# Thirty-four DMA issues of an encoder layer's attention stage, begun by ScalarE instead of SyncE

## The chip, the core and the metric

The kernel is one program on one core of a Trainium2 chip. Its time is the device time of one launch in microseconds (us). The core has a matrix engine (TensorE: PE in the profile, PEld for its weight loads), VectorE (DVE), ScalarE (ACT), GpSimd (POOL) and SyncE (SP). SP computes nothing here: it begins transfers. Each engine works through its own instructions in their order, and an instruction that has to wait holds up all that stand behind it on that engine.

Matrices of weights and activations lie in DRAM. What the engines work on lies in SBUF, and matmuls write to PSUM banks. Whether an engine may go on is told by semaphores that other engines and finished transfers raise.

## What is computed

One layer of a transformer encoder on 1024 tokens of width 1024. Two attention branches of eight heads each (head size 64) are projected, gated, added and projected again. After a layer norm comes a gated feed-forward part.

```python
D_MODEL, SEQ, HEAD_DIM, N_HEADS_A, N_HEADS_B = 1024, 1024, 64, 8, 8
...
        h = x @ w_in[l]
        qa, ka, va, qb, kb, vb, ga, gb = jnp.split(h, split_pts, axis=-1)
        y_a = chunk_band_attention(heads_a(qa), heads_a(ka), heads_a(va), rel_bias[l]) @ w_proj_a[l]
        y_b = stick_breaking_attention(heads_b(qb), heads_b(kb), heads_b(vb)) @ w_proj_b[l]
        gate_a = jax.nn.sigmoid(ga + b_gate[l, :D])
        gate_b = jax.nn.sigmoid(gb + b_gate[l, D:])
        mix = (gate_a * y_a + gate_b * y_b) @ w_out[l]
        x = layer_norm(DEEPNORM_ALPHA * x + mix, ln1_g[l], ln1_b[l])
        g, u = jnp.split(x @ w_ffn_in[l], 2, axis=-1)
        x = layer_norm(DEEPNORM_ALPHA * x + (jax.nn.silu(g) * u) @ w_ffn_out[l], ln2_g[l], ln2_b[l])
```

Branch A is a softmax over a band of nine chunks of 64 keys with a learned bias. Branch B is stick-breaking: a weight is `sigmoid(z)` times the product of `1 - sigmoid(z)` over the keys between, found by a running product.

## The kernel before

All float32 products are made of three fp32r matmuls: each operand is split into a high part (a cast by ACT, L109) and the rest (a subtraction by DVE, L110). The program first projects `x` (to about 345 us of the span), then runs the attention stage (345 to 700 us), the second branch's projection with the output projection and a layer norm (to 830), and the feed-forward part.

**The attention stage** is the loop over `vsteps`: 16 heads (0 to 7 branch A, 8 to 15 branch B), each with 12 steps. A step is a turn (PE transposes up to four 128x128 blocks of weights into a bank `tp`, L561; ACT and DVE split them into `pt`, L109 and L110) and, two steps later, a multiplication (PE multiplies a block of values by `pt` and adds it up in `pv`, L574 and L575). There are three banks for `tp` (in branch B one of them holds the identity for the running products), one for `pv`, four `pt` slots and three `yt` slots. Between the steps the weights of coming heads are made: in branch A scores (L464, L465), bias and minimum on DVE (L495), `exp` on ACT (L500) and scaling on POOL (L503); in branch B two sigmoids on ACT (L528, L529), the running product on DVE (L532, L536) and a product on POOL (L538).

**A head's values** come out in two halves of 512 queries (`g` 0 and 1). Two neighbouring heads share a 128-row tile. After the last multiplication of a half, ACT copies the bank to SBUF (L589: 128x512). One transfer from SBUF to SBUF (L590: 64 rows of 512, 128 KB) brings the rows that belong to the other tile there. Three steps later, POOL adds them up (L593). After the fourth addition of a pair of heads SP stores the tile to `y_dr` (L595). The last pair (`i` = 7) does it otherwise (L581, L582), with no transfer.

**Filling work** is fed between the steps, by a price in matmuls: six gates (10 to 15, `gate()`, L421 on PE, copied by ACT at L424 and stored by one 512 KB transfer each, L425), then branch A's projection (`yAps`, L621). For the latter the stored values come back (`reload_y`: `yraw` by SP at L644, `yh` by ACT at L647, `yl` by POOL at L648), the gates too (`reload_gate`: `gA`, SP at L651, sigmoid by ACT at L653), and weights (`load_w`: SP at L403, ACT at L404, the rest at L405).

**What sets the order.** `dma` is `nc.sync.dma_start` (L83), so that SP begins every transfer before the change. The program is written in one sequence of steps, but a scheduler puts each engine's instructions in an order of its own, and it puts in the semaphore waits. A change to one engine's work therefore moves rows on the others.

Of the kernel before, what the change touches and what calls it, by code (L numbers as in the profile page):

```python
# [18 lines left out]
P = 128  # L19
# [3 lines left out]
DH = 64  # L23
# [24 lines left out]
def hybrid_trunk_kernel(ctx: ExitStack, tc, x, xt, w_in, b_gate, rel_bias, w_proj,  # L48
# [6 lines left out]
    nc = tc.nc  # L55
# [7 lines left out]
    def slot(tag, name, dtype=F32):  # L63
        return pool.tile([P, 1024], dtype, tag=tag, name=name, bufs=SLOTS[tag])
# [10 lines left out]
    def bank(tag, name):  # L75
        return ps.tile([P, HW], F32, tag=tag, name=name, bufs=BANKS[tag])

    def dram(name, n):
        return [dr.tile([P, 1024], F32, name=f"{name}{i}") for i in range(n)]
# [3 lines left out]
    dma = nc.sync.dma_start  # L83
# [13 lines left out]
    g_dr = dram("g_dr", 16)  # L97
# [10 lines left out]
    def split(dst_h, dst_l, src):  # L108
        nc.scalar.copy(dst_h, src)  # L109
        nc.vector.tensor_tensor(dst_l, src, dst_h.bitcast(F32), ALU.subtract)  # L110
# [303 lines left out]
    def gate(i, w):  # L414
        gt = slot("gt", f"gate{i}")
        for hf, cs in enumerate((LO, HI)):
            acc = bank("mm", f"gps{i}_{hf}")
            for k in range(KT):
                ks = slice(k * P, (k + 1) * P)
                for j, (lw, rx) in enumerate(((w[0], xh), (w[0], xl), (w[1], xh))):  # L420
                    mm(acc, lw[:, ks], rx[k][:, cs], start=(k == j == 0),  # L421
                       stop=(k == KT - 1 and j == 2))
                    yield 1.0
            nc.scalar.copy(gt[:, cs], acc)  # L424
        dma(g_dr[i], gt)  # L425

    left(2)
    take = project_plain(0)
# [113 lines left out]
    def value_steps(hd, g, wt):  # L542

        br, h = hd["br"], hd["h"]
        reach = (4, 8)[br]
        q0 = 4 * g
        nm = f"{'ab'[br]}{hd['n']}_{g}"
        pv = []

        kbs = [4, 5, 6, 7, 3, 2, 1, 0] if g == 0 else [7, 6, 5, 4]  # L550
        steps = []
        for i, kb in enumerate(kbs):
            lo_q = max(q0, kb - reach)
            hi_q = min(q0 + 3, kb)
            n = (hi_q - lo_q + 1) * P
            pts = []

            def turn(kb=kb, lo_q=lo_q, hi_q=hi_q, n=n, pts=pts):
                tp = bank("tr", f"tp_{nm}_{kb}")
                for qb in range(lo_q, hi_q + 1):  # L560
                    tr(tp[:, (qb - lo_q) * P:(qb - lo_q + 1) * P],  # L561
                       wt[qb - q0][:, (kb - qb) * P:(kb - qb + 1) * P], ident)
                pt = slot("pt", f"pt_{nm}_{kb}", F32R)
                split(pt[:, 0:n], pt[:, HW:HW + n], tp[:, 0:n])
                pts.append(pt)

            def mult(i=i, kb=kb, lo_q=lo_q, n=n, pts=pts):
                v = hd["v"]
                if i == 0:
                    pv.append(bank("pv", f"pv_{nm}"))  # L570
                last = i == len(kbs) - 1
                cs = slice((lo_q - q0) * P, (lo_q - q0) * P + n)
                pt = pts[0]
                mm(pv[0][:, cs], v[:, kb, :], pt[:, 0:n], start=(i == 0), stop=False)  # L574
                mm(pv[0][:, cs], v[:, kb, :], pt[:, HW:HW + n], start=False, stop=last)  # L575
                if last:
                    yt = hd["yt"]()
                    r = slice(h * DH, (h + 1) * DH)
                    gs = slice(g * HW, (g + 1) * HW)
                    if hd["i"] == 7:  # L580
                        nc.scalar.copy(yt[r, gs], pv[0][DH:P])  # L581
                        nc.vector.tensor_tensor(yt[r, gs], pv[0][0:DH], yt[r, gs], ALU.add)  # L582
                    else:

                        if g == 0:
                            hd["yv"] = slot("yt", f"yv_{nm}")
                        yv = hd["yv"]
                        both, other = (yt, yv) if h == 0 else (yv, yt)
                        nc.scalar.copy(both[:, gs], pv[0])  # L589
                        dma(other[r, gs], both[(DH, 0)[h]:(P, DH)[h], gs])  # L590

                        def add():
                            nc.gpsimd.tensor_tensor(yt[r, gs], yt[r, gs], yv[r, gs], ALU.add)  # L593
                            if h == 1 and g == 1:
                                dma(y_dr[hd["i"]], yt)  # L595
                        later.append([3, add])

            steps.append((turn, mult))
        return steps


    def fill_all():
        w = first_w
        for i in range(first_gate, 16):
            nxt = load_gate(i + 1, nc.gpsimd) if i < 15 else load_proj(0, 0, "op", nc.gpsimd)
            yield from gate(i, w)
            w = nxt
        for i in range(4):
            reload_y(i, nc.gpsimd)
        for cc in range(4):  # L610
            nxt = load_proj(0, cc + 1, "op", nc.gpsimd) if cc < 3 else None
            for j in range(2):
                c = 2 * cc + j
                t = slot("gt", f"gA{c}")
                reload_gate(t, c, 0)
                for hf, cs in enumerate((LO, HI)):
                    acc = bank("mm", f"yAps{c}_{hf}")
                    for k in range(4):
                        ks = slice(j * HW + k * P, j * HW + (k + 1) * P)
                        for n, (lw, rx) in enumerate(((w[0], yh), (w[0], yl), (w[1], yh))):  # L620
                            mm(acc, lw[:, ks], rx[k][:, cs], start=(k == n == 0),  # L621
                               stop=(k == 3 and n == 2))
                            yield 1.0
                    nc.vector.tensor_tensor(t[:, cs], acc, t[:, cs], ALU.mult)
                if c < KEEP:
                    dma(m_dr[c], t)
                else:
                    kept[c] = t
            if cc < 3:
                reload_y(4 + cc, nc.gpsimd)  # L630
            w = nxt
# [484 lines left out]
```

## Time and profile before

| what | value |
|---|---|
| time, median of 3 runs | 1467.64 us (1467.51 to 1469.79) |
| the profiled execution | 1466.33 us |
| its span in the profile | 1464.5 us |
| granted TensorE clock, mean | 0.997 |
| DVE busy | 1035.9 us (71%) |
| DMA | 247.72 MB, 169 GB/s mean |

The profiled execution is 1.31 us under the median. Between its time and its span lie 1.83 us. PE's share is the largest, and it is close to the whole span; so the readings below look for PE's idle time, stretch by stretch, and for what ended it.

### The profile page before, as it was taken

The numbers are of one execution on the slowest core, as the hardware profiler recorded it, in microseconds if no ns is written. First come the engines' busy times: TensorE is split into PE (matmuls) and PEld (weight loads), VectorE is DVE, ScalarE is ACT, GpSimd is POOL, SyncE is SP. The second block draws the span as 40 slices with busy tenths as digits, with TensorE's granted clock in tenths as the row PEclk, the third lists the DMA queues.
The fourth block names the chain that finished last, engine by engine and source line by source line (L and its number), as shares of the span: only waits on it lengthen the run. The fifth ranks groups of instructions, "written<-read, shape, count | busy, mean of one in ns | idle before, by whom it ended". The sixth has DMA issues, their size and how long they took to land.

```text
span 1464.5 us, 19170 instructions
## 1 busy us (share of the span) xinstructions
PE 1429.5 (98%) x6740; PEld 1181.3 (81%) x6740; DVE 1035.9 (71%) x1693; ACT 679.2 (46%) x1179; POOL 278.8 (19%) x326
## 2 busy tenths in 40 slices
PE   8999999999999998999999999999999999999997
PEld 6788888887888787777888888888888888888886
DVE  8856655434776987887848966777776665978767
ACT  6444444334887878775413534444444433221201
POOL 0000000003555779760004100000000000100016
PEclk9999999999999999999999999999999999999999
DMA  6555545328666476747611123444444456886602
GB/s 216 158 188 173 160 142 177 125 100 246 194 191 203 123 224 186 236 170 254 235 43 72 50 95 130 158 154 148 152 151 145 155 190 248 304 306 237 212 15 101
DMA packets 83455, 247.72 MB, mean 169 GB/s; under 512 B 10512, under 2 KB 10512, under 8 KB 83360
## 3 DMA queue, kind: packets, MB, share of 16 engines
q1 hardware_dynamic: 83360, 246.51, 50.6%
q8 instruction: 53, 0.87, 0.2%
q14 instruction: 42, 0.34, 0.1%
HBM read 162.03 MB, written 80.77 MB: 166 GB/s over the span
## 4 chain that ended last, share of the span: by engine, by line
PE 83%; DVE 7%; DMA 4%; ACT 2%; issue 2%; POOL 1%; SPq 0%; POOLq 0%; DVEq 0%; ACTq 0%
PE sxf L171 15%; PE sxp L171 12%; PE szf L171 8%; PE szp L171 6%; PE dx L1049 6%; PE syf L171 4%; PE gps L421 3%; PE dz L1049 3%; PE syp L171 3%; PE ops L119 2%; PE ops L117 2%; PE ops L116 2%; PE yAps L621 2%; PE dy L1049 1%; PE tp_b L561 1%
## 5 line engine op out<-in xcount | busy, mean ns | idle before, releaser
L1005 POOL TENSOR_TENSOR wdyt<-wdyt 128x512 f32<-128x512 f32 x8 | 10.9, 1366 | 513.6 <-DVE wdgt L1004 473.4
L538 POOL TENSOR_TENSOR w_b<-w_b,kp_b 128x511 f32<-128x511 f32 (+3 forms) x96 | 96.8, 1018 | 33.6 <-DVE kp_b L536 28.5
L536 DVE TENSOR_TENSOR_SCAN kp_b<-kp_b,ident_ps 128x384 f32<-128x384 f32 (+6 forms) x88 | 78.4, 891 | 7.0 <-ACT kp_b L528 2.2
L482 POOL MEMSET bias<- 64x64 f32 x8 | 1.2, 144 | 329.2 <-ACT bias L481 329.2
L184 DVE TENSOR_TENSOR c<-sxp,c 128x512 f32<-128x512 f32 x16 | 11.1, 692 | 74.6 <-issue 41.4
L769 POOL TENSOR_TENSOR mv<-mv,neghalf 128x1 f32<-128x1 f32 x16 | 23.8, 1489 | 209.4 <-DVE mv L768 209.4
L528 ACT ACTIVATE kp_b<-sc_b 128x512 f32<-128x512 f32 (+3 forms) x96 | 50.3, 525 | 24.0 <-PE sc_b L465 21.7
L110 DVE TENSOR_TENSOR pt_b<-tp_b,pt_b 128x512 fp32r<-128x512 f32 (+1 forms) x96 | 50.1, 541 | 12.5 <-ACT pt_b L109 12.3
L980 DVE TENSOR_TENSOR x<-dx,x 128x512 f32<-128x512 f32 x64 | 43.5, 687 | 17.0 <-PE dx L1049 16.9
L171 PE MATMUL szf<-x1S63h,wcf 128*128 128x512 f32 x168 | 55.1, 389 | 0.0
L109 ACT CAST pt_b<-tp_b 128x512 fp32r<-128x512 f32 (+1 forms) x96 | 48.4, 517 | 7.9 <-PE tp_b L561 7.3
L110 DVE TENSOR_TENSOR sl<-h,sl 128x512 fp32r<-128x512 f32 x56 | 38.4, 686 | 18.9 <-ACT sl L109 18.9
L503 POOL TENSOR_SCALAR w_a<-w_a,st_a 128x640 f32<-128x640 f32 (+2 forms) x64 | 42.6, 667 | 48.0 <-DVE st_a L502 29.7
L561 PE MATMUL tp_b<-ident,w_b 128*128 128x128 f32 x288 | 47.9, 275 | 3.4 <-DVE pt_b L110 3.1
L110 DVE TENSOR_TENSOR pt_a<-tp_a,pt_a 128x512 fp32r<-128x512 f32 (+1 forms) x96 | 46.0, 487 | 7.1 <-ACT pt_a L109 5.9
L529 ACT ACTIVATE w_b<-sc_b 128x511 f32<-128x511 f32 (+3 forms) x96 | 50.6, 527 | 0.0
L109 ACT CAST sl<-h 128x512 fp32r<-128x512 f32 x56 | 34.7, 619 | 33.5 <-PE syf L171 17.1
L116 PE MATMUL ops<-wh_o,mh 128*128 128x512 f32 x128 | 50.2, 392 | 0.0
L119 PE MATMUL ops<-wh_o,ml 128*128 128x512 f32 x128 | 50.0, 391 | 0.0
L117 PE MATMUL ops<-wl_o,mh 128*128 128x512 f32 x128 | 49.9, 390 | 0.0
L109 ACT CAST pt_a<-tp_a 128x512 fp32r<-128x512 f32 (+1 forms) x96 | 39.9, 425 | 19.2 <-PE tp_a L561 18.3
L500 ACT ACTIVATE w_a<-w_a,st_a 128x640 f32<-128x640 f32 (+2 forms) x64 | 44.7, 698 | 7.4 <-DVE st_a L495 5.7
(1883 smaller groups left out, 4796.5 us busy)
## 6 DMA issues: line engine op xcount, KB each, us to landing
s_dr<-sl SPq DMA_DIRECT2D x112, 256.0 KB, 2.2
sd<-s_dr SPq DMA_DIRECT2D x56, 512.0 KB, 4.8
wLf<-in_w_ffn_in_dram SPq DMA_DIRECT2D x22, 512.0 KB, 4.5
wRf<-in_w_ffn_in_dram SPq DMA_DIRECT2D x22, 512.0 KB, 3.5
wLp<-in_w_in_dram SPq DMA_DIRECT2D x17, 512.0 KB, 5.3
wRp<-in_w_in_dram SPq DMA_DIRECT2D x17, 512.0 KB, 4.2
v_dr<-v SPq DMA_DIRECT2D x16, 512.0 KB, 4.2
qs<-q_dr SPq DMA_DIRECT2D x16, 512.0 KB, 5.0
```

What stands on the lines that cost most here:

```text
L109: nc.scalar.copy(dst_h, src)
L110: nc.vector.tensor_tensor(dst_l, src, dst_h.bitcast(F32), ALU.subtract)
L116: mm(acc, lh, rh, start=(i == 0), stop=False)
L117: mm(acc, lh, rl, start=False, stop=False)
L119: mm(acc, ll, rh, start=False, stop=(i == n))
L171: mm(acc, lw[:, ks], rx, start=(first and kt == i == 0), stop=(kt == 3 and i == 2), skip_group_check=not first)
L528: nc.scalar.activation(kp[:, c0:e], sc[:, 0:n], AF.Sigmoid, scale=-1.0)
L529: nc.scalar.activation(be[:, m0:e], sc[:, m0 - c0:n], AF.Sigmoid)
L536: nc.vector.tensor_tensor_scan(kp[:, s0:e], kp[:, s0:e], ident_ps()[:, 0:e - s0], kp[:, s0 - 1:s0], ALU.mult, ALU.bypass)
L538: nc.gpsimd.tensor_tensor(be[:, m0:e], be[:, m0:e], kp[:, m0 - 1:e - 1], ALU.mult)
L561: tr(tp[:, (qb - lo_q) * P:(qb - lo_q + 1) * P], wt[qb - q0][:, (kb - qb) * P:(kb - qb + 1) * P], ident)
L1049: mm(acc, a, b, start=(first and i == n == 0), stop=(i == n - 1 == 1), skip_group_check=not first)
```

## The change

Two transfers are begun by ACT (`nc.scalar.dma_start`) instead of SP. The bytes, sources and targets are the same.

```diff
@@ gate(i, w)
             nc.scalar.copy(gt[:, cs], acc)
-        dma(g_dr[i], gt)
+        nc.scalar.dma_start(g_dr[i], gt)
@@ value_steps(hd, g, wt), mult()
                         nc.scalar.copy(both[:, gs], pv[0])
-                        dma(other[r, gs], both[(DH, 0)[h]:(P, DH)[h], gs])
+                        nc.scalar.dma_start(other[r, gs], both[(DH, 0)[h]:(P, DH)[h], gs])
```

That is 28 issues of L590 (seven pairs of heads, two heads, two halves) and 6 of L425. Each stands on ACT behind the copy that it reads, at once or a few rows later. SP keeps the stage's other transfers: queries, keys, values, weights, reloads and the remaining stores.

The scheduler's order changes on all engines from the first of these issues on. In the following rows a name ends in a number of its own for each tile; `a6`, `b4` are the head of branch A or B, `+` is a row of the changed kernel and `-` one of before.

ACT at the border of the branches: `w_a7` are the last softmax weights, `kp_b0` and `w_b0` the first sigmoids, and `yt3` holds the values of the pair of heads 6 and 7.

```order
 L500 ACTIVATE w_a7_1_1_4429,st_a7_6_4478<-w_a7_1_1_4429,st_a7_6_4478 128x256
 L589 COPY yt3_4424<-pv_a6_1_4445 128x512
+L590 DMA yv_a6_0_4425<-yt3_4424 64x512
+L500 ACTIVATE w_a7_1_1_4429,st_a7_7_4498<-w_a7_1_1_4429,st_a7_7_4498 128x128
 L528 ACT_TABLE_LOAD
 L528 ACTIVATE kp_b0_0_4510<-sc_b0_0_0_4512 128x512
-L500 ACT_TABLE_LOAD
-L500 ACTIVATE w_a7_1_1_4429,st_a7_7_4498<-w_a7_1_1_4429,st_a7_7_4498 128x128
-L529 ACT_TABLE_LOAD
 L529 ACTIVATE w_b0_0_0_4506<-sc_b0_0_0_4512 128x511
```

The last `exp` now stands ahead of the first sigmoid, so that two of three table loads are gone here.

POOL in head 11, where branch A's projection begins. Before, `yl2` and `yl3` (the rests of the reloaded values) stand ahead of the addition for `yt5`:

```order
L648 TENSOR_TENSOR yl2_5760<-yraw2_5757,yh2_5759 128x1024
L538 TENSOR_TENSOR w_b4_0_0_5653<-w_b4_0_0_5653,kp_b4_0_5657 128x511
L538 TENSOR_TENSOR w_b4_0_0_5653<-w_b4_0_0_5653,kp_b4_0_5657 128x512
L648 TENSOR_TENSOR yl3_5766<-yraw3_5763,yh3_5765 128x1024
L593 TENSOR_TENSOR yt5_5552<-yt5_5552,yv_b2_0_5553 64x512
```

The same place in the changed kernel:

```order
L538 TENSOR_TENSOR w_b4_0_0_5653<-w_b4_0_0_5653,kp_b4_0_5657 128x511
L593 TENSOR_TENSOR yt5_5552<-yt5_5552,yv_b2_0_5553 64x512
L538 TENSOR_TENSOR w_b4_0_0_5653<-w_b4_0_0_5653,kp_b4_0_5657 128x512
L648 TENSOR_TENSOR yl2_5760<-yraw2_5757,yh2_5759 128x1024
L521 MEMSET w_b4_0_3_5656 128x1
L538 TENSOR_TENSOR w_b4_0_1_5654<-w_b4_0_1_5654,kp_b4_1_5704 128x383
L538 TENSOR_TENSOR w_b4_0_1_5654<-w_b4_0_1_5654,kp_b4_1_5704 128x512
L521 MEMSET w_b4_1_0_5880 128x1 x2
L521 MEMSET w_b4_1_1_5881 128x1 x2
L648 TENSOR_TENSOR yl3_5766<-yraw3_5763,yh3_5765 128x1024
```

The addition, which waits for the transfer of L590, has moved ahead of `yl2`; two products for `w_b4` have moved ahead of `yl3`.

PE at that place; `sc_b4` are scores, `tp_b3` transposes, `yAps0` the projection. Before:

```order
L621 MATMUL yAps0_0_5779<-yh3_5765,wh_y0_0_5404 128x512
L464 MATMUL sc_b4_3_0_5834<-kh12_5504,qs12_5502 128x320
L465 MATMUL sc_b4_3_0_5834<-kl12_5507,qs12_5502 128x320
L464 MATMUL sc_b4_3_320_5842<-kh12_5504,qs12_5502 128x320
L465 MATMUL sc_b4_3_320_5842<-kl12_5507,qs12_5502 128x320
L561 MATMUL tp_b3_1_7_5849<-ident_69,w_b3_1_0_5557 128x128 x2
L561 MATMUL tp_b3_1_7_5849<-ident_69,w_b3_1_1_5558 128x128 x2
L621 MATMUL yAps0_0_5779<-yl3_5766,wh_y0_0_5404 128x512
```

And in the changed kernel:

```order
L621 MATMUL yAps0_0_5779<-yh3_5765,wh_y0_0_5404 128x512
L621 MATMUL yAps0_0_5779<-yl3_5766,wh_y0_0_5404 128x512
L621 MATMUL yAps0_0_5779<-yh3_5765,wl_y0_0_5405 128x512
L621 MATMUL yAps0_1_5862<-yh0_5747,wh_y0_0_5404 128x512
L621 MATMUL yAps0_1_5862<-yl0_5748,wh_y0_0_5404 128x512
```

The matmul that reads `yl3` has moved up by six rows, ahead of the scores and transposes.

ACT behind that place, where `yh4` is cast from the reload `yraw4` and `yv_b3` is head 11's copy:

```order
+L653 ACTIVATE gA1_5946<-gA1_5946,bg_76 128x1024
 L109 CAST pt_b3_1_7_5854<-tp_b3_1_7_5849 128x512
-L647 CAST yh4_6110<-yraw4_6108 128x1024
 L109 CAST pt_b3_1_6_5869<-tp_b3_1_6_5865 128x384
 L589 COPY yv_b3_0_5876<-pv_b3_0_5684 128x512
 L528 ACTIVATE kp_b4_4_5882<-sc_b4_4_0_5884 128x512
+L590 DMA yt5_5552<-yv_b3_0_5876 64x512
 L529 ACTIVATE w_b4_1_0_5880<-sc_b4_4_0_5884 128x511
```

The cast of `yh4`, which waits for a reload, no longer stands ahead of the copy; it comes eleven rows behind the L590 of this piece.

## The prediction

> **What bounds the kernel now.** I read the page's busy shares first, then the chain of work that ended last.
>
> ```profile
> PE 1429.5 (98%) x6740; PEld 1181.3 (81%) x6740; DVE 1035.9 (71%) x1693; ACT 679.2 (46%) x1179; POOL 278.8 (19%) x326
> ...
> PE 83%; DVE 7%; DMA 4%; ACT 2%; issue 2%; POOL 1%; SPq 0%; POOLq 0%; DVEq 0%; ACTq 0%
> ```
>
> PE is busy for 98% of the span, and SP's sequencer holds 0% of the chain, so a free SP is worth nothing by itself. The two lines that change run only in the attention stage, so next come the busy times stretch by stretch (PE, PEld, DVE, ACT, POOL, then clock and DMA).
>
> ```profile
> 450.00:500.00 50.00, 46.34 (x265) 37.56 (x264) 39.92 (x99) 43.61 (x101) 33.74 (x49) 1.00 0.59 179
> ...
> 550.00:600.00 50.00, 46.26 (x247) 38.25 (x247) 38.27 (x65) 40.98 (x87) 44.89 (x50) 0.97 0.67 195
> ...
> sum 345.00, PE 327.81 PEld 274.21 DVE 272.72 ACT 263.96 POOL 208.83; mean PE 46.83 PEld 39.17 DVE 38.96 ACT 37.71 POOL 29.83
> ```
>
> From 355 to 700 us PE idles 345 - 327.81 = 17.2 us. That is the ceiling of any gain here (1.2% of the time). ACT has 345 - 263.96 = 81 us without work, but only 6.4 us of 50 in the stretch from 450. The changed issues land on ACT, so the question is whether they fit into those 81 us. What ended PE's idle time in this window (total, times, longest):
>
> ```profile
> PE pv_b L574 <- ACT yv_b L589: 3.1, 1, 3.1
> PE tp_b L561 <- DVE pt_b L110: 3.1, 5, 0.9
> PE pv_b L574 <- ACT yt L589: 2.4, 1, 2.4
> PE pv_b L574 <- DVE yt L582: 1.9, 1, 1.9
> PE tp_a L561 <- DVE pt_a L110: 1.6, 3, 0.8
> ...
> PE sc_a L465 <- DMA kl<-k_dr: 1.5, 1, 1.5
> PE pv_a L574 <- ACT yv_a L589: 0.4, 2, 0.2
> PE pv_a L574 <- ACT yt L589: 0.4, 2, 0.2
> ```
>
> Three single waits (3.1, 2.4, 1.9) make 7.4 us; each ends with a copy out of the one `pv` bank. The only wait for a load is 1.5 us, for keys.
>
> **The moved issues.** The instructions of the two lines as SP ran them (min/median/max in ns):
>
> ```profile
> L590 SPq DMA_DIRECT2D yv_a<-yt x8: 477/477/492, 368.2 to 469.4; - x8
> ...
> DMA to landing us min/median/max: 2.2/2.4/8.9
> ```
>
> ```profile
> L425 SPq DMA_DIRECT2D g_dr<-gate x6: 325/326/577, 396.3 to 566.8; - x6
> ```
>
> 28 x 0.48 + 6 x 0.33 = 15.4 us of issuing leave SP and come to ACT: 18 issues in branch A (16 of L590 up to 491.7 us, 2 stores, 8.3 us) and 16 in branch B (7.1 us). The trace shows no issue by ACT. The nearest row is SP's 0.48; below lies 0 (hidden in ACT's 81 us), above all 15.4 us on PE's path. In branch A PE waited for ACT's copies only 0.4 + 0.4 us, and for `pt_a` only at the border (next part); I let a tenth reach PE, **+0.8**. In branch B it waited for `pt_b` five times and for copies in two of the three long waits; I let a third reach it, **+2.4**. Behind each issue stand the sigmoids and casts of the next steps. These shares are my choice, not a measurement.
>
> What SP gains: it sat at L590 until ACT's work was done, with later loads behind it. But PE waited for a load only at the 1.5 us for keys, at 360 us and so before the first L590 (368.2). I put this at 0.
>
> **The border of the branches.** ACT around 470 us:
>
> ```profile
> 469.42 1.28 ACT L528 ACT_TABLE_LOAD   x1
> 470.71 0.60 ACT L528 ACTIVATE kp_b<-sc_b 128x512 f32<-128x512 f32 x1
> 471.33 1.28 ACT L500 ACT_TABLE_LOAD   x1
> ...
> 473.13 1.28 ACT L529 ACT_TABLE_LOAD   x1
> ```
>
> Sigmoid, `exp`, sigmoid: three loads. With the last `exp` ahead, two go, 2.56 us; one issue of 0.48 comes, so ACT is about 2.1 us ahead from here. PE's waits for `pt_a`, 1.6 us in three, lie at 480 to 486 us, right behind; the ACT casts ahead of DVE's subtraction are late there by less than that. **-1.6** (between 0 and -2.1).
>
> **Head 11.** ACT sat behind a reload:
>
> ```profile
> 572.08 0.62 ACT L109 CAST pt_b<-tp_b 128x512 fp32r<-128x512 f32 x1
> 576.44 1.04 ACT L647 CAST yh<-yraw 128x1024 fp32r<-128x1024 f32 x1 [3.73 <-DMA yraw<-y_dr]
> ...
> 577.76 0.59 ACT L589 COPY yv_b<-pv_b 128x512 f32<-128x512 f32 x1
> ```
>
> The copy PE waited 3.1 us for stood behind this cast. In the new order the cast comes eleven rows behind L590, so this wait goes: -3.1. But POOL's order has changed ahead of it, and PE reads `yl3` earlier. POOL and PE before:
>
> ```profile
> 562.55 2.40 POOL L648 TENSOR_TENSOR yl<-yraw,yh 128x1024 fp32r<-128x1024 f32 x1
> 564.91 2.52 POOL L538 TENSOR_TENSOR w_b<-w_b,kp_b 128x511 f32<-128x511 f32 x2
> 567.40 2.40 POOL L648 TENSOR_TENSOR yl<-yraw,yh 128x1024 fp32r<-128x1024 f32 x1
> 569.77 1.29 POOL L593 TENSOR_TENSOR yt<-yt,yv_b 64x512 f32<-64x512 f32 x1
> ...
> 573.42 1.00 POOL L538 TENSOR_TENSOR w_b<-w_b,kp_b 128x383 f32<-128x383 f32 x1
> ...
> 574.46 1.27 POOL L538 TENSOR_TENSOR w_b<-w_b,kp_b 128x512 f32<-128x512 f32 x1
> ```
>
> ```profile
> 570.25 0.31 PE L464 MATMUL sc_b<-kh,qs 128*128 128x320 f32 x1
> ```
>
> New order from 562.55: two products 2.52, the addition 1.29, `yl2` 2.40, two products 1.00 + 1.27, some 0.2 of memsets, `yl3` 2.40. It ends at 562.55 + 11.1 = 573.6, where before it ended at 569.8. The row that stood behind `yAps0`'s first matmul on `yh3` began at 570.25; there PE now waits for `yl3`, 573.6 - 570.25 = 3.4 us, +3.4. Net **+0.3**. This holds if the addition need not wait, that is if L590's transfer lands by 563.8 (562.55 + 1.26). SP before:
>
> ```profile
> 560.01 0.48 SPq L590 DMA_DIRECT2D yv_b<-yt  x1
> ```
>
> ```profile
> yv_b<-yt SPq DMA_DIRECT2D x1, 128.0 KB, 8.9
> ```
>
> The second row is the DMA view of that moment: this transfer took the 8.9 us and landed at 568.9. From a landing of 2.4 us (median) `yl3` is as worked out; with 8.9 the addition waits 5.1 us more. That bounds this step between -3.1 (POOL ahead of its old times, so that `yl3` isn't waited for) and +0.3 + 5.1 = +5.4. I take the median landing, since half of the 28 are no longer.
>
> The Trainium skill ("DMA: Bandwidth & Descriptors", section "Queues, rings and completion order") has SP and ACT each own one ring on each of the same 16 DMA engines, and an engine goes round between rings packet by packet. By it L590 would not stand behind SP's burst of key loads, so it would land near 2.4 us and the step would be +0.3; by the row of 8.9 us it would be +5.4. No trace so far shows two rings at work.
>
> **Head 12.** The 2.4 us wait stands behind a gate's load:
>
> ```profile
> 586.41 6.75 DMA yt<-yv_b
> ```
>
> ```profile
> 594.63 0.33 SPq L595 DMA_DIRECT2D y_dr<-yt  x1
> ...
> 596.30 0.60 SPq L651 DMA_DIRECT2D gA<-g_dr  x1
> ```
>
> ```profile
> 602.91 1.15 ACT L653 ACTIVATE gA<-gA,bg 128x1024 f32<-128x1024 f32 x1 [2.64 <-DMA gA<-g_dr]
> ```
>
> The first row is from the chain: a transfer of L590 and its time. SP began `gA` only behind the store of `yt5`; the store waited for POOL's addition, and that for this transfer. With L590 landing 2.4 us after its issue, the addition could start at about 589 rather than 593, so the store and `gA` come up to 4 us earlier, against 2.64 us of waiting. **-2.2** (0 if the addition keeps its time, -2.4 at most).
>
> **Head 14.** ACT's cast of `yh6` has moved up, ahead of the last cast of `pt_b6` and of `gA7`'s sigmoid. Before:
>
> ```profile
> 645.01 0.27 ACT L109 CAST pt_b<-tp_b 128x128 fp32r<-128x128 f32 x1 [0.17 <-PE tp_b L561]
> 646.64 1.15 ACT L653 ACTIVATE gA<-gA,bg 128x1024 f32<-128x1024 f32 x1 [1.37 <-DMA gA<-g_dr]
> ...
> 649.43 1.09 ACT L647 CAST yh<-yraw 128x1024 fp32r<-128x1024 f32 x1
> ```
>
> ```profile
> 636.88 2.69 POOL L538 TENSOR_TENSOR w_b<-w_b,kp_b 128x511 f32<-128x511 f32 x2 [2.15 <-DVE kp_b L536]
> ```
>
> If `yraw6` lands as late as its use before, ACT sits 649.4 - 645.0 = 4.4 us there. POOL's addition, on which the store and this reload hang, now stands ahead of the second of these two products, so the reload comes 1.3 us earlier: 3.1 us, in place of the 1.37 at `gA7`, so +1.7. PE's 1.9 us behind `yt` (L582) follow from weights that SP loads right behind the reload; they shrink by the same 1.3. **+0.4** (from -1.9 to +4.4).
>
> **The sum** against the profiled execution, 1466.33: -1.6 + 0.3 - 2.2 + 0.4 + 0.8 + 2.4 = +0.1, so 1466.4. The median of the runs shown is 1.3 above that execution; as a median the sum is 1467.7. Waits leave three places, and others of nearly their size come in.
>
> **The rivals.**
>
> *Faster: the issues are hidden.* For it: ACT's 81 us, and PE's 0.8 us behind copies in branch A. The two shares (+3.2) fall away: -3.1 in all. If POOL also runs ahead, so that `yl3` isn't waited for (3.4 less) and head 14 gives its -1.9 (2.3 less), -8.8. As a median 1459 to 1465.
>
> *Slower: L590's transfer keeps its long landing.* The place is POOL's addition in head 11, now ahead of `yl2` and `yl3`. It decides from a landing later than 563.8 us, and each further us costs PE one. With 8.9 us it is +5.1; in head 14 the same delay takes the 1.3 us from the reload. 0.1 + 5.1 + 1.3 = +6.5: 1474. Against it: the median landing of 2.4 us. For it: two landings in branch B, 8.9 and 6.75 us, were both long. If ACT is also held at half of all issues (7.7 instead of 3.2), +11: 1479.
>
> *Nothing is gained or lost.* The transfer, not its issue, is what is waited for (2.2 us at least against 0.48), and it is the same. Then PE's waits merely change their names: 1467.6, within 2 us. The Trainium skill says so on the page "DMA: Bandwidth & Descriptors", section "Issuing engines are not separate DMA queues": begun by several engines, transfers still run on the same 16 engines, and what is saved is sequencer time, "usually small relative to the DMA itself". The rows of 0.48 and 2.2 us agree.
>
> **How the numbers follow.** About 0.2%, 2.9 us, is what a measurement of this kernel can tell from no change. My forecast has 0.33 (0.27 of it within 0.2%, 0.04 faster, 0.02 slower), hidden issues 0.32 (0.31 faster, 0.01 same), the long landing 0.25 (slower), nothing 0.10 (0.08 same, 0.01 each way). Together: faster 0.36, same 0.36, slower 0.28. The likeliest case alone holds 1464 to 1471. The range goes from 1460 (all but the last part of the faster case, 0.08 left out) to 1477 (past the long landing; 0.1 left out where ACT is held as well).
>
> **What would show it.** Right: one table load near 470 and PE's waits at 480 to 486 gone; no wait of ACT at `yh4` ahead of `yv_b3`'s copy; a PE wait of 3 to 4 us for POOL `yl`; the sigmoid of `gA3` without its 2.64 us. For my shares: PE's waits for `pt_b` grow by 2 to 3 us in all over five, those of branch A by less than 1. The slower rival: POOL waits several us for `yv_b` ahead of `yl2`. The faster one: ACT issues of 0.5 us or less that PE's list of waits doesn't follow. I would be wrong altogether if an issue on ACT took over 1 us, or if PE's idle time changed outside 355 to 700 us.

## The result

| kernel | time, median | runs |
|---|---|---|
| before | 1468.09 us | 1466.72 to 1470.43, 6 runs |
| changed | 1481.55 us | 1476.68 to 1483.49, 6 runs |

The ratio is 1.0084, with a 95% interval of 1.0064 to 1.0103: the change costs 0.84%, some 12 us (the two medians alone differ by 13.5 us). The time lies above the predicted range (1460 to 1477). The profiled execution of the changed kernel took 1476.68 us, 4.9 under its median, with a span of 1474.9 us; its trace shows 10.4 us of the loss.

### The profile page after: what moved, and what is told of

Same layout as the page of the kernel before. It is cut to its first block, busy times and chain, and to the rows that moved or that the text cites. A ratio compares the mean times of both kernels' runs of the same rounds, so it can differ in the third digit from the quotient of the medians.

```text
span 1474.9 us, 19106 instructions
## 1 busy us (share of the span) xinstructions
PE 1434.5 (97%) x6740; PEld 1184.1 (80%) x6740; DVE 1032.1 (70%) x1693; ACT 676.4 (46%) x1177; POOL 277.5 (19%) x326
## 4 chain that ended last, share of the span: by engine, by line
PE 54%; DVE 2%; DMA 1%; POOL 1%; ACT 0%; issue 0%; POOLq 0%; DVEq 0%; ACTq 0%; SPq 0%
PE sxf L171 16%; PE szf L171 8%; PE dx L1049 6%; PE syf L171 4%; PE dz L1049 3%; PE ops L117 2%; PE ops L119 2%; PE ops L116 2%; PE fpswh_h L117 1%; PE dy L1049 1%; PE fpswh_h L119 1%; PE fpswh_h L116 1%; PE yAps L621 1%; PE yBps L116 1%; PE yBps L119 1%; PE yBps L117 1%
## 5 line engine op out<-in xcount | busy, mean ns | idle before, releaser
L529 ACT ACTIVATE w_b<-sc_b 128x511 f32<-128x511 f32 (+3 forms) x96 | 48.4, 504 | 0.3
L561 PE MATMUL tp_a<-ident,w_a 128*128 128x128 f32 x240 | 44.1, 277 | 2.4 <-DVE pt_a L110 1.9
```

The lines of the kernel that those rows point to most:

```text
L529: nc.scalar.activation(be[:, m0:e], sc[:, m0 - c0:n], AF.Sigmoid)
L561: tr(tp[:, (qb - lo_q) * P:(qb - lo_q + 1) * P], wt[qb - q0][:, (kb - qb) * P:(kb - qb + 1) * P], ident)
```

## The profile after

The busy times by stretch, columns as in the prediction, of the changed kernel:

```profile
400.00:450.00 50.00, 42.57 (x248) 36.69 (x247) 29.70 (x113) 31.80 (x82) 23.15 (x32) 0.93 0.63 177
...
550.00:600.00 50.00, 44.13 (x230) 36.69 (x229) 33.35 (x59) 36.44 (x79) 41.25 (x49) 0.90 0.62 198
```

And of the kernel before, the stretch that the prediction didn't show:

```profile
400.00:450.00 50.00, 48.44 (x300) 42.11 (x299) 37.72 (x136) 38.46 (x98) 26.87 (x36) 1.00 0.67 199
```

Two stretches lost, and both show a lower clock. From 400 to 450 us PE worked 42.6 us instead of 48.4, and 0.93 of the clock was granted; that stretch lies in branch A, where the prediction had +0.8 us. What ended PE's idle time between 345 and 715 us:

```profile
PE yAps L621 <- POOL w_b L521: 5.5, 2, 3.2
PE pv_a L574 <- ACT yt L589: 4.1, 2, 3.9
PE sc_a L465 <- DMA kl<-k_dr: 2.5, 1, 2.5
PE tp_b L561 <- DVE pt_b L110: 2.1, 6, 0.7
PE pv_b L574 <- ACT yt L589: 2.1, 1, 2.1
```

The waits of 3.1 us (for `yv_b`) and 1.9 us (for `yt` of L582) are gone. New are 5.5 us in head 11, 3.9 us for a copy in head 3, and 2.5 us for keys. (For the first the view names a memset of POOL, the last row before PE went on; the matmuls read `yl`.)

To see where time was lost I matched the matmuls of both traces and took how much later each started than before (us; the first column is the place in the trace of before):

```
place    changed   all old order,     the same,        before with
                   issue at the copy  one row later    four rows moved
398.5      -1.3         2.5              -0.6             -1.1
410.8       7.6         3.2               0.7             -1.1
471.7       7.0         3.6               0.4             -1.2
481.7       5.3         4.2               0.5             -2.2
491.8       6.4         4.9               0.5             -2.2
552.5       6.7         6.7               0.5             -2.3
593.4      10.5         7.9               1.0             -3.9
645.6      12.1         9.6               3.8             -4.3
655.6      10.1         9.2               4.2             -4.2
726.6      10.3        10.2               4.7             -3.7
```

The changed kernel loses 8.9 us at one place in head 3, gains 1.7 at the border and gives 1.1 back, loses about 4 around head 11 (that is after the 3.1 us wait for `yv_b`, which it no longer has) and gains 2.0 in head 14. The other columns belong to experiments below.

**Head 3.** ACT in the changed kernel:

```profile
400.76 0.59 ACT L109 CAST pt_a<-tp_a 128x512 fp32r<-128x512 f32 x1 [0.28 <-PE tp_a L561]
408.52 1.04 ACT L404 CAST wh_g<-wr_g 128x1024 fp32r<-128x1024 f32 x1 [7.17 <-DMA wr_g<-in_w_in_dram]
...
410.33 0.58 ACT L589 COPY yt<-pv_a 128x512 f32<-128x512 f32 x1
```

The cast of gate 14's weights now stands ahead of the casts and the copy that PE needs; it sat 7.2 us for its load. The gate that uses these weights comes a hundred us later. PE at this place, which waited for keys first and then for the copy:

```profile
404.89 0.38 PE L465 MATMUL sc_a<-kl,qs 128*128 128x320 f32 x1 [2.54 <-DMA kl<-k_dr]
...
410.96 0.79 PE L574 MATMUL pv_a<-pt_a,v 128*128 128x512 f32 x1 [3.87 <-ACT yt L589]
```

The load itself was slow, as the DMA view from 395 to 410 us tells (KB each, us to landing), in the changed kernel:

```profile
kl<-k_dr SPq DMA_DIRECT2D x4, 256.0 KB, 8.0
...
wr_g<-in_w_in_dram SPq DMA_DIRECT2D x1, 512.0 KB, 9.6
v<-v_dr SPq DMA_DIRECT2D x1, 512.0 KB, 8.7
```

and in the kernel before:

```profile
kl<-k_dr SPq DMA_DIRECT2D x4, 256.0 KB, 6.3
...
wr_g<-in_w_in_dram SPq DMA_DIRECT2D x1, 512.0 KB, 5.6
v<-v_dr SPq DMA_DIRECT2D x1, 512.0 KB, 3.5
```

Behind PE's wait comes a second price, the clock (the column ahead of the last two):

```profile
410.00:415.00 5.00, 4.04 (x12) 3.54 (x13) 2.36 (x10) 3.92 (x12) 1.65 (x3) 0.50 0.78 174
415.00:420.00 5.00, 5.00 (x30) 4.70 (x29) 3.15 (x10) 2.58 (x7) 2.34 (x4) 0.82 0.14 39
```

Ten us with 0.50 and 0.82 of the clock are worth about 4.0 x 0.50 + 5.0 x 0.18 = 2.9 us of PE's busy time. With the waits of 2.5 and 3.9 us that makes 9.3, about the 8.9 us lost here.

**Head 11.** POOL in the changed kernel:

```profile
564.05 1.29 POOL L593 TENSOR_TENSOR yt<-yt,yv_b 64x512 f32<-64x512 f32 x1 [2.43 <-DMA yv_b<-yt]
...
569.33 2.40 POOL L648 TENSOR_TENSOR yl<-yraw,yh 128x1024 fp32r<-128x1024 f32 x1
571.70 1.71 POOL L538 TENSOR_TENSOR w_b<-w_b,kp_b 128x127 f32<-128x127 f32 x2
573.37 1.28 POOL L593 TENSOR_TENSOR yt<-yt,yv_b 64x512 f32<-64x512 f32 x1
574.61 1.26 POOL L538 TENSOR_TENSOR w_b<-w_b,kp_b 128x512 f32<-128x512 f32 x1
575.84 2.34 POOL L648 TENSOR_TENSOR yl<-yraw,yh 128x1024 fp32r<-128x1024 f32 x1
...
578.18 2.22 POOL L538 TENSOR_TENSOR w_b<-w_b,kp_b 128x383 f32<-128x383 f32 x2
...
580.51 2.33 POOL L648 TENSOR_TENSOR yl<-yraw,yh 128x1024 fp32r<-128x1024 f32 x1
```

Here `yl1` ends at 571.7, then come two products, the addition, a product, `yl2` (575.8) and two products more before `yl3` (580.5). PE waited for `yl2` (3.2 us) and again for `yl3` (2.4 us). POOL also came to this place late: the addition at 564.05 waited 2.4 us for a transfer of L590, and before the same addition (at 554.47) followed the row ahead of it without a wait.

```profile
575.00:580.00 5.00, 1.83 (x6) 1.48 (x5) 0.00 (x0) 3.76 (x8) 5.00 (x5) 0.73 0.89 277
580.00:585.00 5.00, 2.63 (x7) 1.73 (x6) 0.80 (x2) 0.28 (x2) 5.00 (x8) 0.50 0.39 134
```

**The moved transfers.** L590 in the changed kernel: the issue takes what SP's took, but the landings don't, and POOL waits for them.

```profile
L590 ACTq DMA_DIRECT2D yv_a<-yt x8: 468/471/506, 366.5 to 476.3; - x8
...
  POOL yt L593: 37.0, 14
...
DMA to landing us min/median/max: 2.2/3.9/9.1
```

Before, POOL waited 9.2 us in 6, with a median landing of 2.4 us.

## Theories

**A, the order.** The new order puts rows that wait (ACT's cast in head 3, POOL's addition and products in head 11) ahead of what PE needs. **B, the issue.** ACT is held while it issues. **C, two rings.** SP no longer waits at L590, so its loads begin earlier and run beside ACT's transfers. To tell them apart, most of these kernels keep the order of each engine's rows in the attention stage by a table of numbers: an edge without a semaphore from each row to the next.

```python
for one, then in zip(names, names[1:]):
    tc.add_manual_dep(found[then], one, mybir.DependencyInfo(
        mybir.DependencyClass.NoSync, mybir.DependencyReason.DATA), reason="order")
```

So only the rows shown as moved differ. Each was timed beside runs of the kernel before, and ratios are against those.

## The experiments

**Old order, issues by ACT; and new order, issues by SP.** In the first, PE, DVE, ACT and POOL have the order of before, and the 34 issues stand right behind their copies:

```diff
 L589 COPY yt0_3012<-pv_a0_0_2886 128x512
+L590 DMA yv_a0_0_3013<-yt0_3012 64x512
 L109 CAST pt_a0_1_5_3029<-tp_a0_1_5_3026 128x256
```

> The 34 issues are begun by ACT, as in the change, each right behind the copy that it reads, but PE, DVE, ACT and POOL keep the order of before row by row in the attention stage. Theory A (the new order costs: a cast that waits for a load stands ahead of the copy that PE needs in head 3, and the rests yl2 and yl3 come late on POOL in head 11): the time of before, 1468, within 3 us, and no PE wait of 3 us or more at 400 to 411. Theory B (issuing on ACT costs by itself): about as slow as the change, 1478 to 1484. Theory C (transfers of a second ring slow SP's loads): 1472 to 1482, with L590's median landing near 3.9 us instead of 2.4.

Measured: 1479.76 us, ratio 1.0091 (1.0076 to 1.0106). In the second the two lines say `dma(...)` as before, with the changed kernel's order on the four engines:

> The issues stay with SP, as before, but PE, DVE, ACT and POOL have the changed kernel's order row by row. Theory A: as slow as the change, 1477 to 1484, with PE waiting for yl2 and yl3 in head 11 (3 us and 2 us) and a clock of 0.5 behind it. Theories B and C: near before, 1466 to 1470, since nothing is issued by ACT and there is one ring.

Measured: 1486.1 us, ratio 1.0138 (1.0122 to 1.0155). Both parts cost alone, so theory A alone falls, and so do B and C alone. They also cost more alone than the two together (0.84%), so these two prices can't be added. In the second kernel the cast in head 3 sat even longer:

```profile
415.06 1.04 ACT L404 CAST wh_g<-wr_g 128x1024 fp32r<-128x1024 f32 x1 [12.29 <-DMA wr_g<-in_w_in_dram]
```

SP's own order was left free here, and SP began this load at 406.3 us, behind the keys, instead of 398.8; so the 1.38% isn't what the order costs in the changed kernel. The first kernel's landings had a median of 4.8 us. Its largest wait, 4.0 us in head 14, came with SP's order, which it left free: `gA7` was loaded behind other loads there.

**Undoing the order at two places.** One row of ACT moved in the changed kernel:

```diff
-L404 CAST wh_g14_4739<-wr_g14_4738 128x1024
 L500 ACTIVATE w_a3_1_1_3493,st_a3_6_3542<-w_a3_1_1_3493,st_a3_6_3542 128x256
...
 L109 CAST pt_a3_0_7_3599<-tp_a3_0_7_3597 128x128
+L404 CAST wh_g14_4739<-wr_g14_4738 128x1024
```

> The changed kernel with one row moved: ACT's cast of gate 14's weights (L404, wh_g14) stands eight rows later in head 3, behind that head's first casts and the copy out of the pv bank; all other rows of all engines stay. Theory A (in-order ACT: this cast, waiting 7.2 us for its load, holds the copy that PE needs, and the slow clock behind PE's wait adds to it): 6 to 8 us less than the change, 1472 to 1476, PE's 3.9 us wait for the copy gone, the clock near 1.0 at 410 to 420. Theory C (the load is late because two rings share the DMA engines): the wait only moves to the next rows of ACT, 0 to 2 us less, 1479 to 1482.

Measured: 1474.39 us, ratio 1.0049 (1.0035 to 1.0064). The wait for the copy is gone, and the clock there is 1.00. Then two rows of POOL:

```diff
+L648 TENSOR_TENSOR yl2_5760<-yraw2_5757,yh2_5759 128x1024
+L648 TENSOR_TENSOR yl3_5766<-yraw3_5763,yh3_5765 128x1024
 L538 TENSOR_TENSOR w_b4_0_0_5653<-w_b4_0_0_5653,kp_b4_0_5657 128x511
 L593 TENSOR_TENSOR yt5_5552<-yt5_5552,yv_b2_0_5553 64x512
 L538 TENSOR_TENSOR w_b4_0_0_5653<-w_b4_0_0_5653,kp_b4_0_5657 128x512
-L648 TENSOR_TENSOR yl2_5760<-yraw2_5757,yh2_5759 128x1024
...
-L648 TENSOR_TENSOR yl3_5766<-yraw3_5763,yh3_5765 128x1024
```

> The changed kernel with two rows moved: POOL takes the rests yl2 and yl3 ahead of the first product for w_b4 and of the addition that waits for L590's transfer; all other rows stay. Theory A (POOL's order in head 11 costs PE 3.2 and 2.4 us and the clock behind it): 3 to 6 us less than the change, 1476 to 1479, PE's waits for yl under 2 us in all. Rival: what is taken from yl comes back as late products for w_b4, within 1.5 us of the change.

Measured: 1471.73 us, ratio 1.0033 (1.0020 to 1.0046), more than expected. Then both moves:

> Both moves of the two kernels before in one. Theory A: the two gains add up, 9 to 13 us less than the change, 1468 to 1472, within 3 us of the kernel before. Theory C: no more than 3 us less than the change, 1478 or above. If issuing on ACT (theory B) costs as well, it stays above before by that part, 1471 to 1475.

Measured: 1468.21 us, ratio 1.0004 (0.9993 to 1.0015). Of the change's 0.84%, head 3 is worth 0.35, head 11 0.51, both 0.80. **With three rows put back, nearly the whole loss is gone.** The order isn't the only cause of the loss: in head 3 the load was late as well, and in head 11 POOL was, behind a transfer of L590; the three rows decide whether PE waits for it. The issues stay with ACT in all three kernels, and so do gaps in ACT's work: at about half of the 34 issues ACT sat idle for 0.45 us or more, some 11 us in all, in the changed kernel as with both moves (other waits of ACT included). PE's waits with both moves:

```profile
PE pv_b L574 <- ACT yt L589: 3.5, 1, 3.5
PE sc_a L465 <- DMA kl<-k_dr: 3.3, 2, 2.5
```

The one of 3.5 us is a head later (12), and the keys are still late: what is left looks like theory C. What the new order gains elsewhere, 1.7 us at the border and 1.8 in head 14 by matched matmuls, may pay for that and for the gaps; no kernel takes this apart.

**The price of an issue.** All five engines in the order of before, issues right behind the copies:

> As the first experiment (issues by ACT right behind the copies, order of before on PE, DVE, ACT, POOL), but SP's remaining rows stay in the order of before too. Theory B (each issue holds ACT, in order, for about 0.6 us, and PE follows): the spread cost of the first experiment stays, 6 to 9 us over before, 1474 to 1477; only its 5 us jump in head 14, where SP loaded gate 7's tile later, goes. Theory C (second ring): 1478 or more, as the first experiment. Theory A alone: within 2 us of before.

Measured: 1476.27 us, ratio 1.0058 (1.0040 to 1.0077). ACT at one issue:

```profile
439.63 0.56 ACT L589 COPY yt<-pv_a 128x512 f32<-128x512 f32 x1
440.22 0.49 ACTq L590 DMA_DIRECT2D yv_a<-yt  x1
440.76 0.41 ACT L500 ACTIVATE w_a<-w_a,st_a 128x128 f32<-128x128 f32 x1 [0.57 <-DVE st_a L495]
```

The copy ends at 440.19, the issue starts at 440.22 and ends at 440.71, the next row starts at 440.76: ACT computes nothing for 0.57 us. (The view names DVE as the releaser, but what ended last is the issue.) Over the 34 issues these gaps make 19.0 us, 0.59 each in the median. Next, each issue one row later:

```diff
 L589 COPY yt0_3012<-pv_a0_0_2886 128x512
-L590 DMA yv_a0_0_3013<-yt0_3012 64x512
 L109 CAST pt_a0_1_5_3029<-tp_a0_1_5_3026 128x256
+L590 DMA yv_a0_0_3013<-yt0_3012 64x512
```

> As the experiment with all of the old order, but each of the 34 issues stands one ACT row later, behind the next cast or activation after its copy. Theory B (an issue right behind its copy holds ACT for 0.59 us, since it waits for the copy's end; behind another running instruction it is hidden): the time falls from 1476 to 1467 to 1471, ACT's gap around an issue falls from 0.59 us to about 0.05 to 0.1 where that row was ready, PE's waits for pt_b go back from 6.3 to about 3 us. Theory C (transfers on two rings hinder each other): no such fall, 1474 to 1477, and L590's landings stay between 2.2 and 9 us with a median of 4 us or more.

Measured: 1471.16 us, ratio 1.0024 (1.0014 to 1.0034). ACT at one issue there:

```profile
606.94 0.59 ACT L589 COPY yt<-pv_b 128x512 f32<-128x512 f32 x1
607.41 0.61 ACT L528 ACTIVATE kp_b<-sc_b 128x512 f32<-128x512 f32 x1
607.60 0.47 ACTq L590 DMA_DIRECT2D yv_b<-yt  x1
608.11 0.60 ACT L529 ACTIVATE w_b<-sc_b 128x511 f32<-128x511 f32 x1
```

The next row runs while the sequencer waits for the copy and issues. The median gap fell to 0.03 us (6.6 us in all, other waits included), and 0.34% of the time went with it, while L590's median landing hardly moved (4.3 us, then 4.2): theory B, where the issue stands right behind the copy. Of the 0.58%, 0.24% stayed. The long landings point to theory C, but PE's waits for `pt_b` fell only from 6.3 to 5.2 us and not to the 3 expected, so a rest of theory B isn't excluded.

**Which transfers.** The same, but with one line changed each time. Only L590 by ACT:

> All of the old order; only the 28 transfers of the values' rows (L590) are begun by ACT, one row behind their copies; the stores of the gates (L425) stay with SP. If what is left of the cost (3 us in the experiment one row later) comes from SP no longer waiting at L590, so that its loads are begun earlier and stand beside L590's transfers: 2 to 4 us over before, 1469 to 1472, L590's median landing at 4 us or more. If it comes from the big stores: within 1.5 us of before, landings with a median under 3.5 us.

Measured: 1470.57 us, ratio 1.0026 (1.0015 to 1.0036), median landing 4.1 us. Only L425:

> All of the old order; only the six stores of the gates (L425, 512 KB each) are begun by ACT, one row behind their copies. By the first reading of the experiment beside it: within 1.5 us of before, since SP still waits at each L590 and L590's landings stay at 2.2 to 5 us. By the second: 2 to 4 us over before.

Measured: 1467.09 us, ratio 1.0003 (0.9993 to 1.0014), median landing 2.4 us. So moving the big stores costs nothing that can be measured, and moving the small transfers costs. How, the kernel with the issues one row later shows at the first half of head 10's values. SP, in the kernel before and then in this one:

```profile
550.74 0.48 SPq L590 DMA_DIRECT2D yv_b<-yt  x1
551.28 1.06 SPq L651 DMA_DIRECT2D gA<-g_dr  x2
```

```profile
548.17 0.98 SPq L651 DMA_DIRECT2D gA<-g_dr  x2
```

ACT's issue of L590, and POOL's addition, in the kernel with the issues one row later:

```profile
551.59 0.47 ACTq L590 DMA_DIRECT2D yv_b<-yt  x1
```

```profile
558.06 1.28 POOL L593 TENSOR_TENSOR yt<-yt,yv_b 64x512 f32<-64x512 f32 x1 [3.08 <-DMA yv_b<-yt]
```

Before, SP began L590's transfer ahead of two gate tiles, and it landed in 2.2 us. Now SP no longer waits for the copy, the tiles are begun 3 us earlier, L590's transfer runs beside them and lands in 6.4 us, and POOL's addition waits 3.1 us for it. From there POOL is some 3.5 us late: the store of the tile in head 12 begins at 596.36 instead of 594.63 (only 1.7 later, since before POOL waited 1.8 us ahead of it), the load of `gA3` at 599.24 instead of 596.30, and ACT waits for that:

```profile
605.52 1.15 ACT L653 ACTIVATE gA<-gA,bg 128x1024 f32<-128x1024 f32 x1 [4.27 <-DMA gA<-g_dr]
```

The copy behind this sigmoid is late, and PE waits 4.0 us for it instead of 2.4. With L590 alone moved POOL waits 3.2 us at the same addition. In all kernels with these issues on ACT L590's median landing is 3.8 to 5.1 us, in those with them on SP 2.4 to 3.5. That one chain is seen in the trace; the rest of the 0.24% wasn't followed row by row, and no kernel held SP's loads back while ACT issues.

**Does it beat both?** Theory A says that rows of ACT that wait for a load ahead of a copy cost in the kernel before too. So, with SP issuing everything as before, the `exp` went ahead of the first table load, the casts `yh4` and `gA3` went behind the copies, and POOL's `yl4` behind them:

```diff
-L653 ACTIVATE gA3_6288<-gA3_6288,bg_76 128x1024
 L109 CAST pt_b4_1_6_6179<-tp_b4_1_6_6175 128x384
 L589 COPY yt6_6186<-pv_b4_0_6011 128x512
 L528 ACTIVATE kp_b5_4_6193<-sc_b5_4_0_6195 128x512
 L529 ACTIVATE w_b5_1_0_6191<-sc_b5_4_0_6195 128x511
+L653 ACTIVATE gA3_6288<-gA3_6288,bg_76 128x1024
```

> The kernel before, all issues with SP, with four rows moved: the last exp of branch A ahead of the first table load, the casts of yh4 and of gA3 (which wait for loads) behind the copies out of the pv bank, and POOL's yl4 behind them. Theory A (a row of ACT that waits for a load, ahead of the copy that PE needs, is what costs, whoever begins the transfers): 4 to 8 us less than before, 1459 to 1463, PE's waits of 3.1 and 2.4 us gone, the clock 1.0 at 580. Rival: the waits only move, within 2 us of before.

Measured: 1465.0 us, ratio 0.9984 (0.9975 to 0.9993). The waits of 3.1 and 2.4 us are gone and the clock at 575 to 585 is 1.00; but 0.16%, 2.3 us, came of the 4 to 8 expected: PE's waits for `pt_b` grew from 3.1 to 5.0 us. The same with the issues by ACT:

> The four moved rows and the 34 issues by ACT, one row behind the copies. If hidden issues cost nothing and the transfers don't hinder each other: within 2 us of the experiment with four rows. Theory C: 3 to 8 us slower than that, by waits of ACT or PE for loads that are late.

Measured: 1469.78 us, ratio 1.0013 (1.0004 to 1.0023), 0.29% above the kernel with four rows moved. Of PE's waits those for keys grew by 2.0 us, which is of theory C's kind, and those for `pt_b` by 2.3, which may be of either kind. Last, two rows more in head 14, SP issuing:

```diff
-L404 CAST wh_y1_3_7063<-wr_y1_3_7062 128x1024
 L581 COPY yt7_6783<-pv_b6_0_6629 64x512
 L528 ACTIVATE kp_b7_4_6789<-sc_b7_4_0_6791 128x512
 L529 ACTIVATE w_b7_1_0_6787<-sc_b7_4_0_6791 128x511
+L404 CAST wh_y1_3_7063<-wr_y1_3_7062 128x1024
```

> The kernel before with the four moved rows, and two more in head 14: ACT's cast of wh_y1_3, which waits for its load, behind the copy of L581, and DVE's subtraction for it behind the addition of L582. Theory A: PE's wait of 1.9 us for that addition goes, 1 to 2 us less than with four rows, 1463 to 1464. Rival: the work moved stands in the way of the next casts, no change from 1465.

Measured: 1463.8 us, ratio 0.9981 (0.9973 to 0.9990), the fastest kernel of this study. Its interval overlaps that of the one with four rows, so the last step isn't shown to be a gain of its own: the wait of 1.9 us is gone, but those for `pt_b` grew from 5.0 to 5.9 us.

## Why the prediction was wrong

The forecast was no change; the loss is 0.84%. Point by point:

- **The moved issues, branch A (+0.8).** This step failed. I priced the issues of branch A and not the rows that had moved there: head 3's cast had gone ahead of the copy, and I had looked for such moves only where PE already waited. It was worth 0.35%, 5.1 us, by the wait of 3.9 us and the slow clock behind it; of the wait for keys 2.3 us stayed.
- **The moved issues, branch B (+2.4).** The price of an issue was right (0.47 us against 0.48). PE's waits for `pt_b` fell in the changed kernel, from 3.1 to 2.1 us, and didn't grow. The full price of ACT being held, 0.34%, shows only where each issue stands right behind its copy.
- **What SP gains (0).** The sign was wrong. A free SP begins its loads earlier, beside L590's transfers, and both land later. Three comparisons put this at 0.24 to 0.29%, with whatever is left of ACT's being held.
- **The border (-1.6).** Right in mechanism, too large: two table loads went and PE was 1.7 us earlier at 481.7, but 1.1 came back by 491.8. The waits at 482 to 492 stayed, 0.6, 0.8, 0.3 and 0.5 us. About -0.6.
- **Head 11 (+0.3).** The waits came as worked out in kind: none for `yv_b`, one for `yl3`. Mis-sized: a wait for `yl2` came as well, 5.5 us in all instead of 3.4. I let POOL come to this place at its old time; against PE's rows it came some 2.5 us later, since the addition ahead waited 2.4 us for L590's transfer. And there is the clock behind the waits, which I had left out although before's row of that stretch had 0.97. Putting POOL's two rows back was worth 0.51%, 7.5 us.
- **Head 12 (-2.2).** Failed: PE still waited 2.1 us for that copy. The term rested on L590 landing in 2.4 us; the transfer was issued at 597.6, and POOL's addition waited for it until 604.1.
- **Head 14 (+0.4).** Better than forecast: 2.0 us gained, within the bounds given. ACT waited 1.1 us for `yh6`'s reload there, not 3.1.
- **The rivals.** The slower one had the right mechanism in part (long landings, POOL's addition ahead of the rests); I gave it a quarter, and put it at 1474 to 1479. It lacked head 3 and the clock.

On the pages cited: from the Trainium skill ("DMA: Bandwidth & Descriptors", section "Queues, rings and completion order") I had taken that a ring of ACT's own lets L590 land near 2.4 us. The landings of 4 to 9 us in about half of the cases say otherwise. Going round between rings shares the 16 engines; it gives no right of way to the small transfer. The other section, "Issuing engines are not separate DMA queues", agrees with the rows in that two queues shared the engines (from 395 to 410 us one had 78.0% and the other 17.9% of their time); that only sequencer time is at stake isn't what the runs show, since an order between transfers was lost too.

## What to carry to other kernels

When an issue moves to another engine, read the whole new order, not only the places where something waits today: look for each row that waits for a load or for another engine's last step, and ask what that PE needs stands behind it. A sequencer that waits is also a gate on the transfers behind it; taking the wait away puts those beside the transfer that it waited for. In this kernel an issue by a computing engine was best placed one row behind what it reads, so that another instruction runs while it waits and issues.

## What was not expected of the hardware

- **The clock behind a wait of PE.** After a wait of 3.9 us the granted clock was 0.50 and then 0.82 in the next ten us, and one 128x512 matmul took 0.79 us instead of about 0.40. That wait thus cost 2.9 us more than the idle time in PE's list. The waits don't sort by length alone: one of 2.5 us left the clock at 1.00 in the changed kernel (404.9 us), and one of the same length lowered it to 0.66 in its five us with both moves (405.6 us); one of 1.94 us in head 14 left it at 1.00 before (655 to 660 us) and was followed by 0.66 in the kernel with all of the old order (665 to 670 us). These means fit stretches of 3.4 us, or twice that, at half rate (an estimate: 0.34 x 5 / 0.5 = 3.4). The Trainium skill ("TensorE: Matmul & The Clock Gate", section "What's actually happening") has a gate that drops to half rate after an idle window of some 3.4 us and comes back after a busy one, with windows that run freely. The 3.9 us and the way back over some 3.4 us or more agree; the waits of 2.5 and 1.94 us with a drop behind them are shorter than the window, and where the limit lies wasn't tried.
- **A small transfer beside large ones.** 128 KB from SBUF to SBUF land in 2.2 us at best (at 550.7 us before, ahead of the gate tiles) and in 4 to 9 us in half of the recorded cases of the changed kernel (6.4 us behind the same tiles); one 512 KB load in head 3 went from 5.6 to 9.6 us.
- **Hidden issues.** An issue by ACT is nearly free (0.03 us of gap in the median) behind a running instruction and costs 0.59 us behind the one whose end it waits for.
